# Expert results of two pairs of experts accumulated in one PSUM bank, and added to the rows after the gate and up products instead of between their steps

## The chip, the cores and the metric

The kernel runs on one core of a Trainium2 chip. Its metric is the device time in microseconds (us) of one execution. Names of engines: PE is TensorE's matmuls, PEld its weight loads, DVE is VectorE, ACT is ScalarE, POOL is GpSimd, SP is SyncE, which issues most transfers.

## What is computed

Two blocks follow each other on 512 tokens of 1024 features. The first (two layers of pooling, retention and RWKV branches) and the attention of the second are the same on both sides of the change. The change is in the mixture of experts at the end: 32 experts, of which every token uses two.

```python
def _hierarchical_moe(xt, w_rg, b_rg, w_re, b_re, w_gate, w_up, w_down):
...
    y = jnp.zeros_like(xt)
    for e in range(N_EXPERTS):
        he = jax.nn.silu(xt @ w_gate[e]) * (xt @ w_up[e])
        y = y + combine[:, e:e + 1] * (he @ w_down[e])
    return y
...
        x = x + y.reshape(B, T, D)
    return _rmsnorm(x, final_norm)
```

An expert has 1024 x 256 gate weights, as many up weights, and 256 x 1024 down weights, all float32.

## The kernel before

The experts' stage (`experts`, `pairs`) takes the last sixth of the span. The tokens were sorted to their experts beforehand: an expert has 64 places (`CAP`), and a pair of experts fills the 128 partitions, so there are n = 16 pairs. `pairs` goes over them, and PE's instructions keep the order in which the code is written (the call of `pairs` stands under `manual_schedule` for PE); for the other engines a scheduler chooses the order. For each pair p the code does this:

- `one_hots`, `places` (lines 1693 to 1701): for the pair three further on, which tokens lie at its 128 places, their weights `ws` and their rows `idx`; an indirect transfer from POOL (`rows`, line 1705) then fetches the 128 rows of 1024 features into `xg`. On PE this is four small matmuls (line 1682), on DVE the two reductions `ws` (1686) and the cast `idx` (1690).
- `gate_up` (1731): 8 steps of two matmuls (line 1737) with 64 columns of stationary operand each, one for each expert of the pair, into the halves of one bank `pp`. The trace shows each as two records, so the whole product is 32. After them tanh on ACT (1741) and two DVE instructions (1742, 1743) make the hidden values `eth`.
- `turned` (1708): four transposes (1712) and an ACT copy (1714) give `ohT`, the one-hots turned, that is, the matrix that takes an expert's places back to tokens.
- `gather` (1717): twice four transposes (1725) and a DVE multiply (1728) give `xt`, the next pair's rows with the features on the partitions. The code stops between its two halves.
- `transposed` (1746): two transposes of `eth` (1750) and an ACT copy `eht` (1752).
- `down` (1755): two halves of four matmuls (1762), 16 records in all, and for each half the weighted result in two parts, `hi` by ACT (1765) and `lo` by DVE (1766). These four tiles of 128 x 512 are the `ys` of the pair; they lie in buffers with the tag `y`.
- `add` (1769): a generator of 8 steps, one for each block of 128 tokens and each half of the features. A step is two matmuls (line 1775: `ohT` block as stationary operand, `hi` then `lo`) into one of two banks `mm`, and a DVE instruction (1777) that adds the bank to the tokens' rows `xr`.

The generator `add` of a pair is run one step at a time between the 8 steps of the next pair's `gate_up`:

```python
            for _ in self.gate_up(2 * p, x, wts):
                next(add, None)
...
            ys = list(self.down(2 * p, pl[p][1], ht, wts))
            add = self.add(oT[p], ys)
```

The last pair (p = 15) is written out behind the loop: its `gate_up` runs alone, with a branch at its fifth step (`rest`, for tokens past an expert's capacity), and the steps of pair 14's `add` stand around its `down`.

Weights come from SP's queue. Five buffers each hold an expert's gate and up weights (`eg`, 2 MB) and down weights (`ed`, 1 MB). A buffer is refilled when the products that read it are done: the refills of `eg` wait for the end of a `gate_up`, those of `ed` for the end of a `down`.

Of the kernel before, what the change touches and what calls it, by code (L numbers as in the profile page):

```python
# [33 lines left out]
# columns of the packed parameters of a layer, 128 features to a column  # L34
# [8 lines left out]
# 128-wide feature tiles of w_in, in the order in which they are used  # L43
# [21 lines left out]
# constants that follow from the shapes alone  # L65
def _consts():
# [28 lines left out]
    # for the second block  # L95
# [7 lines left out]
    # biases of the distances 511 .. -128: one-hot bucket, log of the number of dilations with the distance  # L103
# [26 lines left out]
def _groups(w, g=128):  # L130
    """[K, N] -> [128, N/g, K/128, g]"""
    K, N = w.shape
    return w.reshape(K // 128, 128, N // g, g).transpose(1, 2, 0, 3)


def _pack(a):
# [25 lines left out]
    # second block  # L162
# [17 lines left out]
class Layers:  # L180
    """The first block, with the features on the partitions and the tokens along the free axis."""

    def __init__(self, ctx, tc, a, dbg=None):
# [6 lines left out]
        # pools of the first block; those on the right side also serve the second  # L190
# [10 lines left out]
        # what only the first block needs  # L201
# [65 lines left out]
    def rsqrt(self, src, n, scale, eps, out=None, own=""):  # L267
        """(src * scale + eps) ** -0.5 on [128, n] by Newton's iteration"""
# [20 lines left out]
    def load(self, dst, src):  # L289
        """behind the loads that the start waits for"""  # L290
        if self.after is None:
            self.nc.sync.dma_start(dst, src)
        else:
            with self.tc.issue_after(self.after.ins):
                self.nc.sync.dma_start(dst, src)
# [12 lines left out]
    def mm3(self, ps, w, h, start=True, stop=True):  # L308
        """ps += w.T @ h, of parts (hi, lo): hi hi + hi lo + lo hi"""
# [8 lines left out]
    def parts(self, src, scale=1.0, tile=None):  # L318
        """hi and lo of a [128, 512] tile"""
# [11 lines left out]
    def dense(self, src, h):  # L331
        """[128 features, 512 tokens] in PSUM: src.T @ h for weights [128, k, 128] in DRAM"""
        p = self.P()
        self.mm3(p, self.split(self.load_w(src)), h)
        return p
# [28 lines left out]
    def mod_params(self):  # L364
        """silu(c) and the layers' parameters"""
# [19 lines left out]
    def mod_start(self, half):  # L385
        """the columns of silu(c) @ w_ada + b_ada that a half of the first norm's features needs"""
        nc, a = self.nc, self.a
        pc, mod, sc = self.mods[0]
        # rows of 512 columns on the partitions 0, 32 and (of every other 128 features) 64, 96, then turned into columns
# [21 lines left out]
    def mod_rest(self):  # L411
        """the other columns, a tile of features at a time"""
# [18 lines left out]
    def rstd_row(self, ss):  # L431
        """[128, 512] in PSUM: 1 / rms of the tokens, the same on all partitions; ss are parts of the sum of squares"""
# [23 lines left out]
    def modnorm(self, xs, rb, sc, sh):  # L456
        """hi and lo of x * rb * sc + sh; x is overwritten"""
# [17 lines left out]
    def rwkv_proj(self, l, h, tiles):  # L475
        """projections p + (p of the token before - p) * mu"""
# [25 lines left out]
    def both(self, *gens):  # L502
        """the generators step by step together"""
# [27 lines left out]
    def to_row(self, s):  # L531
        """[128 tokens, (block, head)] -> [4 heads, 512 tokens]"""
# [8 lines left out]
    def rwkv_prep(self, l, hf, r, k, v, wa):  # L541
        """scaled operands of the chunked recurrence"""
# [19 lines left out]
        for i in range(2):  # L562
# [27 lines left out]
            # k * (1 + (a - 1) * k_a)  # L590
# [23 lines left out]
        # half of (bonus * v + ln_b)  # L614
# [9 lines left out]
        # products of a chunk, masked, by way of DRAM: rows B|K, columns A|R; a unit is a chunk of a head  # L624
# [16 lines left out]
        # B and K times the decay from the token to the chunk's end  # L641
# [7 lines left out]
        # inverses of the diagonal blocks of 32, a block to a partition  # L649
# [27 lines left out]
    def rwkv_chain(self, l, AR, BT, v, bv, DC, gd, tn):  # L677
# [4 lines left out]
        def operands(ch):  # L682
            # operands of the chunk
# [42 lines left out]
        for ch in range(NC_):  # L726
# [10 lines left out]
            # the chunk  # L737
# [64 lines left out]
    def layernorm(self, y, g, eps, tile, own):  # L802
        """in place on [128, 512] of g groups: (y - mean) * rstd"""
# [14 lines left out]
    def silu2(self, ps):  # L818
        """2 * silu of a PSUM tile"""
# [12 lines left out]
    def branch(self, l, n, o, h, acc, gates=()):  # L832
        """acc += 2 * sigmoid(gate logits) * (o @ w_branch)"""
# [18 lines left out]
    def pool_mixer(self, l, h, pc):  # L852
        """causal window means, less the token itself; a map per group; gated"""
# [41 lines left out]
    def rows_of(self, src, h, tile, scale=None):  # L895
        """[128 tokens, 512 features] tiles of the product with four tiles of weights"""
# [27 lines left out]
    def rope_tables(self):  # L924
        """cos and signed sin of the positions times the frequencies"""
# [8 lines left out]
        # ang - 2 pi n, with 2 pi in four parts that take few bits each  # L934
# [103 lines left out]
    def layer(self, l, h, xnext):  # L1038
        """returns the next x and the sum of its squares by partition"""
# [38 lines left out]
        for d in range(8):  # L1078
# [10 lines left out]
            if l == 1:  # L1089
                ss2 = self.sumsq(ss2, x, self.pv2[:, d:d + 1])  # L1090
                # parts of x * final_g * attn_norm for the second block; its norms follow the products
# [51 lines left out]
class Second(Layers):  # L1143
    """The second block: attention, then the experts, with the tokens on the partitions."""

    def second_block(self, xs, ss, ss2, out):
# [11 lines left out]
        # norms of the two blocks' ends: rs1 of x, rs2 of x * rs1 * final_g  # L1158
# [7 lines left out]
        # rs1 = (s1 + eps) ** -0.5, rs1 * rs2 = (s2 + eps * (s1 + eps)) ** -0.5  # L1166
# [53 lines left out]
    def bcast_tokens(self, rs):  # L1220
        """[128, 512] in PSUM from [128 tokens, 4]: the same on all partitions"""
# [18 lines left out]
    def x_rows(self, xs, rs1):  # L1240
        """the first block's result with the tokens on the partitions"""
# [14 lines left out]
    def gates(self, h):  # L1256
        """-cumsum(log sigmoid(f)) of the heads, to DRAM"""
# [23 lines left out]
        # log(1 + exp(-|z|)) = 2 atanh(u), u = (1 - t) / (3 + t), t = tanh(|z| / 2)  # L1281
# [613 lines left out]
```

## Time and profile before

| | us |
|---|---|
| median of 3 runs | 2035.27 |
| fastest and slowest of them | 2031.1, 2045.47 |
| span of the profiled execution, first to last instruction | 2034.7 |

The profile gives the span of its execution and not the time of the call; of the three runs the median is the nearest, 0.57 us above that span, and this is taken as what lies around it. In the rows, "idle before" is an engine's waiting time and the arrow says what ended it; a row of the timeline merges neighbouring instructions of one kind (x16), and its start is that of the first. Matmuls are pipelined, so that the recorded durations of two neighbours overlap: how fast they follow each other is read from their starts.

### The profile page before, as it was taken

To read this page: it belongs to the slowest core of one execution; us is meant where nothing else is said; L and a number is where in the kernel's file an instruction comes from. 1 tells how busy PE (TensorE), PEld (TensorE's weight loads), DVE (VectorE), ACT (ScalarE), POOL (GpSimd) and SP (SyncE) were. 2 spreads that over 40 slices of the span, in tenths; PEclk is the share of its full clock that TensorE was granted. 3 is DMA by queue.
4 is the path that set the end of the run, shared out by engine and by line. 5 is a ranking of instruction groups with operands and counts; after the bars stand their busy time and mean duration, and the time that the engine had idled before them with its cause. 6 is when DMAs were issued, how large, how long until landed. Compare 5 with 4: busy or idle time off the path is not lost. (4 is left out here: it accounts for less than half of the span.)

```text
span 2034.7 us, 26175 instructions
## 1 busy us (share of the span) xinstructions
PE 1924.1 (95%) x10034; PEld 1399.2 (69%) x10034; DVE 1130.2 (56%) x2353; ACT 594.5 (29%) x1054; POOL 538.3 (26%) x444
## 2 busy tenths in 40 slices
PE   6899889999999989979999999999999998999996
PEld 3778667878887867767778888787787686333332
DVE  4656977763334555587674334375564545455445
ACT  3332223233322333213233323352343432111112
POOL 1342454335537411224221232310101221000000
PEclk9899889999999989989999999999999798999999
DMA  7424313443333622421233232345231245888981
GB/s 297 135 88 120 107 48 95 138 118 115 117 97 127 214 68 74 133 82 56 76 108 102 73 95 68 91 136 173 73 104 52 100 188 221 346 362 343 367 320 53
DMA packets 103127, 289.02 MB, mean 142 GB/s; under 512 B 31112, under 2 KB 44296, under 8 KB 94808
## 3 DMA queue, kind: packets, MB, share of 16 engines
q1 hardware_dynamic: 97912, 267.40, 38.7%
q0 software_dynamic: 5088, 19.93, 2.6%
q8 instruction: 80, 1.31, 0.3%
q14 instruction: 47, 0.39, 0.1%
HBM read 268.90 MB, written 21.01 MB: 142 GB/s over the span
## 5 line engine op out<-in xcount | busy, mean ns | idle before, releaser
L313 PE MATMUL mm<-hi,whi 128*128 128x512 f32 x1424 | 575.8, 405 | 26.5 <-DVE ry L966 10.5
L313 PE MATMUL mm<-hi,wlo 128*128 128x512 f32 x1424 | 568.7, 400 | 3.2 <-DVE wlo L305 2.9
L313 PE MATMUL mm<-lo,whi 128*128 128x512 f32 x1424 | 569.7, 400 | 1.6 <-DVE lo L326 1.1
L313 PEld LDWEIGHTS mm<-hi,whi 128*128 128x128 f32 x1424 | 272.1, 191 | 98.6 <-issue 12.7
L302 ACT ACTIVATE whi<-wst 128x1024 fp32r<-128x1024 f32 (+1 forms) x202 | 192.9, 957 | 487.4 <-PE mm L313 354.9
L313 PEld LDWEIGHTS mm<-hi,wlo 128*128 128x128 f32 x1424 | 272.4, 191 | 68.2 <-DVE wlo L305 5.9
L313 PEld LDWEIGHTS mm<-lo,whi 128*128 128x128 f32 x1424 | 272.7, 191 | 65.9 <-issue 6.3
L305 DVE TENSOR_TENSOR wlo<-wst,whi 128x1024 fp32r<-128x1024 f32 (+1 forms) x162 | 186.3, 1152 | 146.5 <-ACT whi L302 144.8
L305 POOL TENSOR_TENSOR wlo<-wst,whi 128x1024 fp32r<-128x1024 f32 (+1 forms) x40 | 86.4, 2161 | 355.6 <-ACT whi L302 260.9
L1737 PE MATMUL pp<-eg,xt 128*64 128x512 f32 x512 | 136.0, 618 | 0.2 <-PEq L1785 0.2
L1777 DVE TENSOR_TENSOR xr<-xr,mm 128x512 f32<-128x512 f32 x128 | 87.3, 685 | 87.0 <-PE mm L1775 86.7
L419 POOL TENSOR_TENSOR wad<-wad,cact 128x1024 f32<-128x1024 f32 x32 | 67.5, 2111 | 147.0 <-DMA wad<-wada 138.6
L1775 PEld LDWEIGHTS mm<-y,ohT 128*128 128x128 f32 x256 | 38.3, 188 | 98.8 <-DVE xr L1777 72.7
L1775 PE MATMUL mm<-y,ohT 128*128 128x512 f32 x256 | 92.5, 446 | 1.9 <-DVE xr L1777 1.9
L421 POOL TENSOR_TENSOR wad<-wad 128x512 f32<-128x512 f32 (+2 forms) x96 | 90.1, 939 | 6.0
L915 PE MATMUL mm<-vhi,hi 128*128 128x256 f32 x256 | 75.9, 301 | 6.8 <-ACT vhi L909 4.2
L1705 POOL DMA_INDIRECT xg<-hx,idx x16 | 15.5, 966 | 240.8 <-DVE oh L1552 204.1
L915 PE MATMUL mm<-vlo,hi 128*128 128x256 f32 x256 | 75.2, 296 | 0.6 <-DVE vlo L910 0.6
L915 PE MATMUL mm<-vhi,lo 128*128 128x256 f32 x256 | 74.9, 294 | 0.0
L847 POOL TENSOR_TENSOR acc<-acc,tg 128x512 f32<-128x512 f32 x32 | 49.9, 1560 | 94.2 <-DVE tg L845 65.2
L1737 PEld LDWEIGHTS pp<-eg,xt 128*64 128x64 f32 x512 | 28.3, 137 | 54.3 <-issue 54.0
L663 DVE TENSOR_TENSOR tmp<-tt,lt 64x31 f32<-64x31 f32 (+15 forms) x124 | 57.4, 463 | 6.1 <-DMA lt<-gd 3.6
(409 smaller groups left out, 2858.3 us busy)
## 6 DMA issues: line engine op xcount, KB each, us to landing
wst<-win SPq DMA_DIRECT2D x154, 512.0 KB, 3.8
eg<-egu SPq DMA_DIRECT2D x31, 2048.0 KB, 13.5
ed<-edn SPq DMA_DIRECT2D x31, 1024.0 KB, 11.0
wad<-wada SPq DMA_DIRECT2D x48, 512.0 KB, 4.8
wst<-wbr SPq DMA_DIRECT2D x48, 256.0 KB, 2.8
gd<-gs SPq DMA_DIRECT2D x64, 128.0 KB, 1.9
gt<-gd SPq DMA_DIRECT2D x32, 256.0 KB, 3.1
wst<-wout SPq DMA_DIRECT2D x16, 512.0 KB, 4.1
```

The lines of the kernel that those rows point to most:

```text
L302: nc.scalar.activation(hi, w, AF.Copy)
L305: e.tensor_tensor(lo, w, hi.bitcast(F32), op=OP.subtract)
L313: self.nc.tensor.matmul(ps, w[x][:, k, :], h[y][k], start=start and k == 0 and i == 0, stop=stop and k == n - 1 and i == 2)
L419: nc.gpsimd.tensor_tensor(w, w, self.cact.unsqueeze(2).to_broadcast([128, 8, 128]), op=OP.mult)
L421: nc.gpsimd.tensor_add(w[:, :n], w[:, :n], w[:, n:2 * n])
L663: nc.vector.tensor_tensor(t, tt[:, 0:j + 1, j:j + 1].to_broadcast([2 * nu, j + 1, n]), lt[:, j:j + 1, j + 1:].to_broadcast([2 * nu, j + 1, ...
L847: nc.gpsimd.tensor_add(acc[d], acc[d], t)
L915: nc.tensor.matmul(p[:, :256], h[x][k][:, tb * 128:tb * 128 + 128], parts[y][k // 2][:, k % 2, :], start=k == 0 and i == 0, stop=k == 7 an ...
L1705: self.last_row = self.nc.gpsimd.indirect_dma_start(xg, None, self.hx[:, :], bass.IndirectOffsetOnAxis(ap=idx, axis=0))
L1737: nc.tensor.matmul(p[64 * i:64 * i + 64], x[:, k, 64 * i:64 * i + 64], wts[e + i][0][:, k], start=k == 0, stop=k == 7)
L1775: nc.tensor.matmul(p, oT[:, 128 * tb:128 * tb + 128], y, start=i == 0, stop=i == 1)
L1777: nc.vector.tensor_tensor(xr, xr, p, op=OP.add)
```

## The change

Results of two pairs, p - 1 and p with p odd, are added together. A step of `add` now has four matmuls into one bank (hi and lo of the one pair, hi and lo of the other) and still one DVE instruction. The 8 steps of such a double are taken four at a time, with all of them behind `gate_up`, `places` and the first half of `gather`: four in the next pair (first half of the features), four in the one after it (second half). Pair 14 takes all eight steps of pairs 12 and 13. The results of pairs 14 and 15 are added by themselves around and behind the last pair's `down`, as before. `turned` moves behind the add steps. The `y` buffers go from 6 to 8, the `eth` buffers from 2 to 1. Comments and docstrings are left out too, and line numbers from 1642 on move by 4 to 6 (1737 is 1741 after the change, 1775 is 1781, 1777 is 1783).

```diff
-        add = iter(())
+        add, ys = iter(()), []
         for p in range(n - 1):
             if p + 3 < n:
                 oh = self.one_hots(p + 3)
             for _ in self.gate_up(2 * p, x, wts):
-                next(add, None)
+                pass
             ht = self.hidden
             if p + 3 < n:
                 pl.append(self.places(p + 3, oh))
-            if p:
-                oT.append(self.turned(pl[p + 1][0]))
             x = self.gather(pl[p + 1])
             next(x)
+            for _ in range(4 if p < n - 2 else 8):
+                next(add, None)
+            if p:
+                oT.append(self.turned(pl[p + 1][0]))
             ht = self.transposed(ht)
             x = next(x)
-            ys = list(self.down(2 * p, pl[p][1], ht, wts))
-            add = self.add(oT[p], ys)
+            ys.append(list(self.down(2 * p, pl[p][1], ht, wts)))
+            if p % 2:
+                add = self.add(zip(oT[p - 1:p + 1], ys[p - 1:p + 1]), True)
             if p == n - 3:
                 self.flag = nc.values_load(self.flag[0:1, 0:1], min_val=0, max_val=T)
+        add = self.add([(oT[n - 2], ys[n - 2])])
...
-        for _ in self.add(oT[p], ys, True):
+        for _ in self.add([(oT[p], ys)], True):
             pass
...
-        th = self.S("eth", [128, 256], "eth", 2)
+        th = self.S("eth", [128, 256], "eth", 1)
...
-            hi, lo = (self.S("y", [128, 512], "y", 6, F32R) for _ in range(2))
+            hi, lo = (self.S("y", [128, 512], "y", 8, F32R) for _ in range(2))
...
-    def add(self, oT, ys, halves=False):
+    def add(self, pairs, halves=False):
+        pairs = list(pairs)
         for tb, c in sorted(((tb, c) for tb in range(4) for c in range(2)), key=lambda i: i[::-1] if halves else i):
             p = self.P()
-            for i, y in enumerate(ys[c]):
-                nc.tensor.matmul(p, oT[:, 128 * tb:128 * tb + 128], y, start=i == 0, stop=i == 1)
+            parts = [(oT, y) for oT, ys in pairs for y in ys[c]]
+            for i, (oT, y) in enumerate(parts):
+                nc.tensor.matmul(p, oT[:, 128 * tb:128 * tb + 128], y, start=i == 0, stop=i == len(parts) - 1)
             xr = self.xr[tb][:, 512 * c:512 * c + 512]
             nc.vector.tensor_tensor(xr, xr, p, op=OP.add)
             yield
```

The order of PE's instructions shows where the add steps stand. Before the change, around the end of one pair's gate and up products (`pp`), the last step of the previous pair's adds (`mm`) follows the last products, and the small matmuls of the next pair's preparation come behind it:

```order
L1737 MATMUL pp_15042<-eg_14043,xt_15004 64x512
L1737 MATMUL pp_15042<-eg_14047,xt_15004 64x512
L1775 MATMUL mm_15087<-y_15036,ohT_14892 128x512
L1775 MATMUL mm_15087<-y_15037,ohT_14892 128x512
L1682 MATMUL ms_15095<-cwx_13543,oh_15040 128x6 x4
L1712 MATMUL rm_15107<-ident,oh_14820 128x128 x4
L1725 MATMUL rm_15115<-ident,xg_14885 128x128 x4
L1750 MATMUL qy_15121<-ident,eth_15091 128x128 x2
L1725 MATMUL rm_15126<-ident,xg_14885 128x128 x4
```

After the change, at the same place on PE, the products end without an add, the preparation comes first, and then the first of four add steps, now of four matmuls with two `ohT`:

```order
L1741 MATMUL pp_15064<-eg_14051,xt_14995 64x512
L1741 MATMUL pp_15064<-eg_14055,xt_14995 64x512
L1686 MATMUL ms_15085<-cwx_13543,oh_15062 128x6 x4
L1729 MATMUL rm_15098<-ident,xg_14891 128x128 x4
L1781 MATMUL mm_15104<-y_14854,ohT_14725 128x512
L1781 MATMUL mm_15104<-y_14855,ohT_14725 128x512
L1781 MATMUL mm_15104<-y_14956,ohT_14827 128x512
L1781 MATMUL mm_15104<-y_14957,ohT_14827 128x512
```

Three more such steps follow it on PE, into the banks `mm_15110`, `mm_15116` and `mm_15122`, and only then the turned one-hots, the transposes of `eth`, the second half of the gather and the down products:

```order
L1781 MATMUL mm_15122<-y_14956,ohT_14827 128x512
L1781 MATMUL mm_15122<-y_14957,ohT_14827 128x512
L1716 MATMUL rm_15128<-ident,oh_14858 128x128 x4
L1754 MATMUL qy_15135<-ident,eth_15081 128x128 x2
L1729 MATMUL rm_15140<-ident,xg_14891 128x128 x4
L1766 MATMUL ms_15146<-ed_14052,eht_15138 64x512
```

On DVE, before the change, the additions to `xr` stand between the steps and the last one between the two instructions that make `eth`:

```order
L1777 TENSOR_TENSOR xr_11110<-xr_11110,mm_14641 128x512
L1742 SCALAR_TENSOR_TENSOR eth_14651<-eth_14651,pp_14602 128x256
L1777 TENSOR_TENSOR xr_11110<-xr_11110,mm_14647 128x512
L1686 TENSOR_REDUCE ws_14660<-ms_14655 64x1 x2
L1743 TENSOR_TENSOR eth_14651<-eth_14651,pp_14602 128x256
L1690 CAST idx_14663<-ms_14655 128x1
L1552 TENSOR_TENSOR oh_14710<-pm_13542,cst_10905 128x512
L1728 TENSOR_TENSOR xt_14674<-rm_14675,pv_82 128x512
```

After the change DVE makes `ws`, `idx`, the first half of `xt` and `eth` first, and the four additions of the pair stand together behind them:

```order
L1690 TENSOR_REDUCE ws_14682<-ms_14677 64x1
L1746 SCALAR_TENSOR_TENSOR eth_14673<-eth_14673,pp_14656 128x256
L1690 TENSOR_REDUCE ws_14682<-ms_14677 64x1
L1694 CAST idx_14685<-ms_14677 128x1
L1732 TENSOR_TENSOR xt_14689<-rm_14690,pv_82 128x512
L1747 TENSOR_TENSOR eth_14673<-eth_14673,pp_14656 128x256
L1783 TENSOR_TENSOR xr_11107<-xr_11107,mm_14696 128x512
L1783 TENSOR_TENSOR xr_11108<-xr_11108,mm_14702 128x512
L1783 TENSOR_TENSOR xr_11109<-xr_11109,mm_14708 128x512
L1783 TENSOR_TENSOR xr_11110<-xr_11110,mm_14714 128x512
L1552 TENSOR_TENSOR oh_14756<-pm_13542,cst_10905 128x512
L1732 TENSOR_TENSOR xt_14689<-rm_14732,pv_82 128x512
```

The transfers keep their order on SP and POOL, and ACT's instructions keep theirs.

## Rows read from the trace of the kernel before

**Rows 1.** Busy time by engine, granted clock, DMA share and GB/s, 50 us of the stage.

```profile
1850.00:1900.00 50.00, 49.01 (x216) 19.10 (x216) 25.95 (x49) 6.84 (x13) 2.80 (x3) 1.00 0.86 340
```

**Rows 2.** Costliest groups: line, engine, names, count, busy and mean ns, idle before and releasers.

```profile
L1777 DVE TENSOR_TENSOR xr<-xr,mm 128x512 f32<-128x512 f32 x128 | 87.3, 685 | 87.0 <-PE mm L1775 86.7
L1775 PEld LDWEIGHTS mm<-y,ohT 128*128 128x128 f32 x256 | 38.3, 188 | 98.8 <-DVE xr L1777 72.7
L1775 PE MATMUL mm<-y,ohT 128*128 128x512 f32 x256 | 92.5, 446 | 1.9 <-DVE xr L1777 1.9
```

**Rows 3.** Timeline of one pair, down product to down product: start, length, engine, line.

```profile
1840.66 3.65 PE L1762 MATMUL ms<-ed,eht 128*64 128x512 f32 x16
...
1844.14 1.03 PE L1737 MATMUL pp<-eg,xt 128*64 128x512 f32 x4
...
1845.10 0.73 PE L1775 MATMUL mm<-y,ohT 128*128 128x512 f32 x2
...
1845.77 1.08 PE L1737 MATMUL pp<-eg,xt 128*64 128x512 f32 x4
...
1846.77 0.73 PE L1775 MATMUL mm<-y,ohT 128*128 128x512 f32 x2
...
1857.39 0.50 PE L1682 MATMUL ms<-cwx,oh 128*128 128x6 f32 x4
...
1857.75 0.66 PE L1712 MATMUL rm<-ident,oh 128*128 128x128 f32 x4
...
1858.24 0.60 PE L1725 MATMUL rm<-ident,xg 128*128 128x128 f32 x4
...
1858.44 0.60 ACT L1714 ACTIVATE ohT<-rm 128x512 fp32r<-128x512 f32 x1 [1.10 <-PE rm L1712]
...
1859.14 0.44 PE L1750 MATMUL qy<-ident,eth 128*128 128x128 f32 x2 [0.29 <-DVE eth L1743]
...
1859.61 0.38 ACT L1752 ACTIVATE eht<-qy 128x256 f32<-128x256 f32 x1 [0.57 <-PE qy L1750]
...
1860.05 2.37 PE L1762 MATMUL ms<-ed,eht 128*64 128x512 f32 x10
```

**Rows 4.** Timeline of PE in the dense products: first and twelfth of 12 neighbours.

```profile
1484.04 0.39 PE L313 MATMUL mm<-lo,whi 128*128 128x512 f32 x1
...
1486.54 0.39 PE L313 MATMUL mm<-hi,whi 128*128 128x512 f32 x1
```

**Rows 5.** Timeline of PE in the last pair: two add steps without a product between.

```profile
2010.92 1.19 PE L1775 MATMUL mm<-y,ohT 128*128 128x512 f32 x4
...
2012.04 1.94 PE L1762 MATMUL ms<-ed,eht 128*64 128x512 f32 x8
```

**Rows 6.** Timeline behind pair 0's gate and up products, which have no adds.

```profile
1720.81 0.61 PE L1682 MATMUL ms<-cwx,oh 128*128 128x6 f32 x4
...
1721.28 0.66 PE L1725 MATMUL rm<-ident,xg 128*128 128x128 f32 x4
...
1722.82 0.41 DVE L1743 TENSOR_TENSOR eth<-eth,pp 128x256 f32<-128x256 f32 x1
...
1724.25 3.65 PE L1762 MATMUL ms<-ed,eht 128*64 128x512 f32 x16
```

**Rows 7.** As rows 1, while transfers stream without a gap.

```profile
1744.00:1758.00 14.00, 14.00 (x56) 4.12 (x52) 6.17 (x9) 1.37 (x2) 0.41 (x1) 1.00 1.00 417
```

**Rows 8.** SP's issues of weights in the timeline, and their landing from the page.

```profile
1837.52 0.80 SPq L1613 DMA_DIRECT2D eg<-egu  x2
...
1856.91 0.81 SPq L1613 DMA_DIRECT2D eg<-egu  x2
...
eg<-egu SPq DMA_DIRECT2D x31, 2048.0 KB, 13.5
```

**Rows 9.** As rows 1, before pair 0's products and in the wait behind them.

```profile
1710.40:1715.40 5.00, 4.97 (x16) 2.57 (x18) 1.38 (x2) 0.00 (x0) 0.41 (x1) 0.51 0.99 363
...
1722.00:1723.00 1.00, 0.00 (x0) 0.00 (x0) 0.99 (x4) 0.00 (x0) 0.00 (x0) 1.00 0.83 164
```

More of the change, by code (lines that the diff above doesn't have):

```diff
@@ L1649, in pairs @@
                 pl.append(self.places(p + 3, oh))
+            x = self.gather(pl[p + 1])
+            next(x)
+            for _ in range(4 if p < n - 2 else 8):
+                next(add, None)
             if p:
                 oT.append(self.turned(pl[p + 1][0]))
-            x = self.gather(pl[p + 1])
-            next(x)
             ht = self.transposed(ht)
             x = next(x)
-            ys = list(self.down(2 * p, pl[p][1], ht, wts))
-            add = self.add(oT[p], ys)
+            ys.append(list(self.down(2 * p, pl[p][1], ht, wts)))
+            if p % 2:
+                add = self.add(zip(oT[p - 1:p + 1], ys[p - 1:p + 1]), True)
             if p == n - 3:
                 self.flag = nc.values_load(self.flag[0:1, 0:1], min_val=0, max_val=T)
+        add = self.add([(oT[n - 2], ys[n - 2])])
         p = n - 1
```

## The prediction, made before the changed kernel was run

> **What bounds the kernel now.** I read the busy time by stretches first. In the experts' stage PE is busy 49.0 of 50 us at a granted clock of 1.00, DVE 26.0 and ACT 6.8, and the DMA engines carry 0.86 of what they can [rows 1]. So PE sets the pace and the transfers run close behind it. The costliest groups come next [rows 2]. DVE's additions look expensive (128 of them, 87.3 us, and 87.0 us of waiting before them), but it is DVE that waits for PE. PE's weight loads show 72.7 us of waiting "for DVE", yet the matmuls themselves waited 1.9 us for it: a load that stands behind a running product has nothing to do, and the row names the last event it saw. Taking additions off DVE is therefore worth nothing by itself. What counts is how close together PE's instructions stand, and for that I read the timeline of one pair by its start times [rows 3].
>
> A pair takes 19.39 us, from one down product to the next (1840.66 to 1860.05). The down product is 16 records in 3.48 us (1840.66 to 1844.14), 0.2175 us each. A step of the gate and up product is 4 records of the same shape, so 0.87 us alone. But a step together with its add step takes 1.67 us (1845.10 to 1846.77): 0.67 for the two adds (to 1845.77) and 1.00 for the four records. Two matmuls of the add's shape (128x128 stationary, 512 columns) need far less when they follow each other: eleven of them take 2.50 us in the dense products, 0.2275 each [rows 4]. So a step should cost 0.87 + 0.455 = 1.325, and the other 0.35 us is the price of going from one tile shape to the other and back, eight times per pair. The last pair shows it from the other side: four adds in a row take 1.12 us (2010.92 to 2012.04) [rows 5], which is 4 x 0.2275 plus 0.21 for going in and out.
>
> **The change part by part.** Matmuls: 224 add matmuls run in the loop before and after, 16 per pair on average. Nothing is removed on PE; what goes is the alternation. DVE loses 56 of 128 additions, 56 x 0.685 = 38 us of busy time, all of it beside PE's work: counted as 0.
>
> Now one pair from 2 to 13, with the end of the gate and up product as zero. The products take 2 x 3.48 = 6.96 us without the adds. The small matmuls of the next places start at once, the first half of the gather at 0.47 (1720.81 to 1721.28 where no add stood in between [rows 6]); four transposes take 0.49 (1857.75 to 1858.24 [rows 3]), so the adds start at 0.96. A step is 4 x 0.2275 = 0.91, with 0.10 once for going in: steps end at 1.97 and 2.88. The third step needs the first bank back. DVE has the two `eth` instructions, `ws`, `idx` and `xt` queued ahead of its additions; in pair 0 that chain ended 2.42 after the products (1722.82 + 0.41 - 1720.81 [rows 6]). So the first addition runs from 2.42 to 3.10, PE waits 0.22, steps three and four end at 4.05 and 4.96, and the second bank (free at 3.79) holds up nothing. A DVE addition takes 0.69 against 0.91 for a step, so DVE does not become the pace.
>
> This wait is new. Behind it on PE stand `turned`, the transposes of `eth`, the second half of the gather and the down product. `eth` is long ready by then, so today's wait for it (0.29 on PE [rows 3]) goes. But `turned` now stands directly before the transposes, and on ACT its copy `ohT` stands before `eht`: `ohT` starts 0.69 after the transposes (1857.75 to 1858.44) and takes 0.60, so `eht` starts at 4.96 + 0.69 + 0.60 = 6.25 at the earliest, and the down product 0.44 after that (1859.61 to 1860.05), at 6.69. The pair takes 6.96 + 6.69 + 3.48 = 17.13 us, 2.26 less than now; 12 pairs give 27.1.
>
> Pair 1 loses its adds altogether. Its tail is that of pair 0, 3.44 from the products to the down product (1720.81 to 1724.25 [rows 6]), so 13.88 in place of 19.39: 5.5 gained. Pair 14 has eight steps: 17.13 + 16 x 0.2275 = 20.77, 1.4 lost. The last pair's program is the same. Sum: 27.1 + 5.5 - 1.4 = 31.2 us, to be taken from the profiled execution's own time, 2034.7 of span and 0.6 around it, which is the median of the runs: 2004.1 us.
>
> What I cost at nothing: the `y` buffers (the next pair's four results fit into the four that its first-half adds have just freed, so ACT and DVE do not wait for later adds; without that cover the additions would wait behind `lo` on DVE), and the single `eth` buffer (its last reader is a whole product away from its next writer). `oh` and the second half of `xt` stand behind the four additions on DVE, some 2.8 us later than today, covered by the 3.48 us of the down product and the first four steps of the next one. The indirect fetch from POOL is issued after `idx`, which stays ahead of the additions, and its rows are wanted two pairs later. On SP the order stays; the `eg` refills are issued at the end of the products, which now comes some 6 us earlier within the pair.
>
> **Whether the weights keep up** is the term that no row shows directly, because today they wait for PE. A pair moves 2 x 2048 + 2 x 1024 KB of weights and 512 KB of rows, 6.82 MB; at 417 GB/s, measured over 14 us with the engines full [rows 7], that is 16.4 us. From the other side, 340 GB/s at a share of 0.86 [rows 1] makes 395 when full, 17.25 us, which is 0.1 over my pair. Refills issued at 1856.91 land 13.5 later, 1870.4 [rows 8]; the product that needs them starts 2 x 19.39 behind 1844.14, at 1882.9. That lead of 12.5 us covers 12 x 0.1. I take no loss, and keep the other end for the range.
>
> The Trainium skill ("DMA: Bandwidth & Descriptors", Where 436 GB/s comes from) speaks against this: it holds that loads from HBM are bound at about 358 GB/s per core, which by an estimate from that figure would be 19.05 us per pair, hardly below today. The trace does not bear it out: 417 GB/s stand in rows 7.
>
> **Rivals.** (1) The weights set the pace. If the transfers cannot do better on average than today's 6.82 MB in 19.39 us (352 GB/s), pair 14 can start only as much earlier as the lead allows, 12.5, minus 1.4: 2024 us; if they do slightly better, 18.6 us per pair (366 GB/s), another 9 us come: 2015. I put this case at 2020. For it: the share of 0.86. Against it: rows 7. (2) Standing together does not help: the adds keep 0.33 us each, as between the products now. Then a pair's adds take 5.3 instead of 3.6 us, the 12 pairs gain 0.6 each, pair 14 loses 4.7: 7 + 5.5 - 4.7 = 8, so 2027. For it: the add reloads 128 columns of `ohT` for every matmul. Against it: rows 4 do so too, at 0.2275, and rows 5. (3) Slower than before: the clock. PE's new waits in each pair (0.22 for the bank, about 0.5 for `eht`) make the granted clock fall at each pair, and it comes back only after some 5 us of work, as at the stage's start, where it was 0.51, the lower of the two levels, over 5.0 us [rows 9]. That loses 5.0 x 0.49 = 2.45 us in each of 14 pairs, 34.3 in all: 2004.1 + 34.3 = 2038. It decides from 31.2 / 14 = 2.2 us per pair on. Against it: pair 0 has a wait of over a microsecond at the same place (1722 to 1723, PE not busy at all) at a clock of 1.00 [rows 9], and the products behind it ran at full pace.
>
> The Trainium skill ("TensorE: Matmul & The Clock Gate", A second HAM failure mode) describes rival 3: a PE that idles briefly between groups while it cycles through PSUM banks can swing between its two clocks. By that rule the result would be the 2038 of rival 3; rows 9 show no fall behind a longer wait, so I give it little.
>
> **How the numbers follow.** Forecast 0.76, weights 0.10, no gain from standing together 0.07, clock 0.07. The forecast's own range: with neither the bank's wait (0.22) nor that for `eht` (0.33) it is 12 x 0.55 = 6.6 lower, 1997.5; with DVE's chain 1 us later than in pair 0 it is 12 higher, 2016. The three runs lie within 0.7% of each other, so about 1% (20 us) is what a measurement of this kernel can tell from no change. The range 1996 to 2016 takes in the forecast and the better end of rival 1. Faster by over 1% (below 2015): nearly all of the forecast and a third of rival 1, 0.78. Within 1%: the rest of rival 1, rival 2 and most of rival 3, 0.17. Slower by over 1%, if the clock stays low for longer than 5 us per pair: 0.05.
>
> **What would show it.** SP's `eg` refills come every 17.1 us instead of 19.4; between two of them 32 product records take about 7.0 us, 16 add matmuls about 3.9; the additions' count is 72. A wait of PE on a transfer within the products means rival 1, add records 0.33 apart within a step mean rival 2, a granted clock below 1.00 between 1750 and the last pair rival 3. PE waiting for DVE at every add step, and not only at the third, would make the forecast wrong in its largest term.

## The result, and the profile after

The changed kernel takes 2006.69 us (median of 4 runs, 2002.31 to 2011.46) against 2037.9 us (4 runs, 2031.1 to 2045.47) for the kernel before beside it: a ratio of 0.9844, 95% interval 0.9814 to 0.9875. The profiled execution took 2007.01 us, 2005.2 of it span. The prediction was 2004.1 us in 1996 to 2016. The two medians differ by 31.2 us, to the digit what was forecast; that closeness is luck, since executions of one kernel lie up to 14 us apart (2031.1 to 2045.47).

The busy time by stretches, in the columns of [rows 1], for two stretches of the stage after the change:

```profile
1750.00:1800.00 50.00, 48.74 (x244) 24.32 (x242) 21.20 (x42) 7.89 (x15) 2.81 (x3) 1.00 1.01 424
...
1850.00:1900.00 50.00, 48.71 (x244) 24.27 (x242) 21.18 (x42) 7.88 (x15) 2.81 (x3) 1.00 0.99 402
```

PE is no busier than in [rows 1] (48.7 of 50 us, before 49.0), but it gets through 244 matmul records in the time in which it got through 216. The clock stays at 1.00. DVE falls from 26.0 to 21.2. The transfers have gone from a share of 0.86 to about 1.00: in the same time they bring more weights, and that stands nearly at what they can do.

The costliest groups, which answer to [rows 2], and the landing of the weights, which answers to [rows 8] (from the page):

```profile
L1781 PE MATMUL mm<-y,ohT 128*128 128x512 f32 x256 | 69.2, 409 | 3.2 <-DVE xr L1783 1.6
...
L1781 PEld LDWEIGHTS mm<-y,ohT 128*128 128x128 f32 x256 | 44.8, 188 | 23.3 <-DVE xr L1783 13.2
...
eg<-egu SPq DMA_DIRECT2D x31, 2048.0 KB, 14.4
```

The 256 add matmuls are all still there, at 69.2 us of busy time instead of 92.5. The idle time before their weight loads fell from 98.8 to 23.3 us, but that is not what was gained: the matmuls themselves show 1.9 us of waiting before and 3.2 now, a little more. A refill of weights takes 0.9 us longer to land (14.4 against 13.5).

One pair in the timeline, which answers to [rows 3]:

```profile
1843.17 3.65 PE L1766 MATMUL ms<-ed,eht 128*64 128x512 f32 x16 [0.31 <-ACT eht L1756]
...
1846.66 7.04 PE L1741 MATMUL pp<-eg,xt 128*64 128x512 f32 x32
...
1853.62 0.61 PE L1686 MATMUL ms<-cwx,oh 128*128 128x6 f32 x4
...
1854.50 4.33 PE L1781 MATMUL mm<-y,ohT 128*128 128x512 f32 x16
...
1855.97 1.34 DVE L1783 TENSOR_TENSOR xr<-xr,mm 128x512 f32<-128x512 f32 x2
1856.71 1.69 PEld L1781 LDWEIGHTS mm<-y,ohT 128*128 128x128 f32 x8 [0.55 <-DVE xr L1783]
...
1858.67 0.60 PE L1716 MATMUL rm<-ident,oh 128*128 128x128 f32 x4
...
1859.31 0.60 ACT L1718 ACTIVATE ohT<-rm 128x512 fp32r<-128x512 f32 x1 [5.16 <-PE rm L1716]
...
1859.80 0.38 ACT L1756 ACTIVATE eht<-qy 128x256 f32<-128x256 f32 x1
...
1860.23 1.08 PE L1766 MATMUL ms<-ed,eht 128*64 128x512 f32 x4 [0.31 <-ACT eht L1756]
```

A pair takes 17.06 us (1843.17 to 1860.23) where it took 19.39. The 32 product records follow each other for 6.96 us, and the 16 add matmuls stand in one block. What holds the block up is seen in the loads: the second eight start at 1856.71, right behind DVE's first addition (1855.97 + 0.69 = 1856.66), which frees their bank. Then `ohT` and `eht` follow on ACT, and the down product waits 0.31 us for `eht`.

SP's first issue of an `eg` refill stands at the end of pair 0's products, and the program ahead of it is the same in both kernels. Of before, the timeline of SP's queue:

```profile
1720.91 1.06 SPq L1613 DMA_DIRECT2D eg<-egu  x2
```

and of after:

```profile
1723.65 1.06 SPq L1613 DMA_DIRECT2D eg<-egu  x2
...
1751.43 0.80 SPq L1613 DMA_DIRECT2D eg<-egu  x2
...
1921.91 0.33 SPq L1613 DMA_DIRECT2D eg<-egu  x1
```

From this refill to the end of the span before took 2034.7 - 1720.91 = 313.8 us, after 2005.2 - 1723.65 = 281.55: the stage gained 32.2 us. The profiled execution gained only 29.5, since its unchanged first part happened to be 2.7 us longer. I call this length the stage below, and the distance of two refills the period ((1921.91 - 1751.43) / 10 = 17.05 us after the change). In all the kernels here but the one with full tiles (whose pair 0 itself takes longer) the start of the stage lies anywhere from 1713.95 to 1729.85, up to 16 us apart, so a single run's total says little and these two say much. Stage and period are of one profiled execution each; where no number of runs is given below, the kernel was run once.

### The profile page after: what moved, and what is told of

It is laid out like the page before. It is cut to its first block, busy times and chain, and to the rows that moved or that the text cites. A ratio compares the mean times of both kernels' runs of the same rounds, so it can differ in the third digit from the quotient of the medians.

```text
span 2005.2 us, 26106 instructions
## 1 busy us (share of the span) xinstructions
PE 1897.0 (95%) x10034; PEld 1417.7 (71%) x10034; DVE 1092.4 (54%) x2297; ACT 592.9 (30%) x1054; POOL 539.2 (27%) x444
## 5 line engine op out<-in xcount | busy, mean ns | idle before, releaser
L1741 PE MATMUL pp<-eg,xt 128*64 128x512 f32 x512 | 114.6, 600 | 0.2 <-PEq L1791 0.2
L1741 PEld LDWEIGHTS pp<-eg,xt 128*64 128x64 f32 x512 | 37.1, 139 | 74.5 <-issue 74.2
L1781 PE MATMUL mm<-y,ohT 128*128 128x512 f32 x256 | 69.2, 409 | 3.2 <-DVE xr L1783 1.6
L1766 PE MATMUL ms<-ed,eht 128*64 128x512 f32 x256 | 58.7, 599 | 4.2 <-ACT eht L1756 4.0
L1781 PEld LDWEIGHTS mm<-y,ohT 128*128 128x128 f32 x256 | 44.8, 188 | 23.3 <-DVE xr L1783 13.2
## 6 DMA issues: line engine op xcount, KB each, us to landing
eg<-egu SPq DMA_DIRECT2D x31, 2048.0 KB, 14.4
```

What stands on the lines that cost most here:

```text
L1741: nc.tensor.matmul(p[64 * i:64 * i + 64], x[:, k, 64 * i:64 * i + 64], wts[e + i][0][:, k], start=k == 0, stop=k == 7)
L1766: nc.tensor.matmul(py[64 * i:64 * i + 64], ht[:, 128 * k + 64 * i:128 * k + 64 * i + 64], wts[e + i][1][:, k, 512 * c:512 * c + 512], star ...
L1781: nc.tensor.matmul(p, oT[:, 128 * tb:128 * tb + 128], y, start=i == 0, stop=i == len(parts) - 1)
```

## The experiments

My theory: what costs is PE going from one tile shape to the other and back, 0.35 us each time, eight times per pair before the change and once now; and four matmuls per bank keep DVE off the pace. Seven times 0.35 is 2.45 us per pair, of which 19.39 - 17.05 = 2.34 are seen. Rivals: the gain comes from fewer additions on DVE; or from where the block stands; or weights, not PE, set the period by now.

**The move alone.** Two matmuls per bank as before, but all eight add steps behind the products:

```diff
             for _ in self.gate_up(2 * p, x, wts):
-                next(add, None)
+                pass
...
-            if p:
-                oT.append(self.turned(pl[p + 1][0]))
             x = self.gather(pl[p + 1])
             next(x)
+            for _ in add:
+                pass
+            if p:
+                oT.append(self.turned(pl[p + 1][0]))
```

> Only the place changes: each pair's 8 add steps of two matmuls stand together behind the gate and up products, and every step keeps its own DVE addition. If the alternation of tile shapes is all that cost time, a pair takes the 17.05 us of the changed kernel. My theory has a second half: 8 additions of 0.67 us behind a DVE chain that ends 2.4 us after the products let the bank of the last step free only at about 6.4, so the adds end near 6.9 and not 5.05, and a pair takes about 18.9 us, some 2028 us in all. If only the number of additions counts, a pair stays at 19.4.

2028.14 us (before beside it 2036.03), period 19.30, stage 2026.4 - 1714.20 = 312.2 us: 1.6 us gained and no more. The direction is the one expected, but a pair takes 0.4 us more than the 18.9 expected; that the total meets the expected 2028 is luck, as this run's stage began 6.7 us earlier than that of the kernel before. PE and DVE in the timeline of this kernel:

```profile
1846.88 1.33 PE L1777 MATMUL mm<-y,ohT 128*128 128x512 f32 x4 [1.03 <-DVE xr L1779]
1848.39 1.33 PE L1777 MATMUL mm<-y,ohT 128*128 128x512 f32 x4 [0.18 <-DVE xr L1779]
...
1846.14 1.28 DVE L1779 TENSOR_TENSOR xr<-xr,mm 128x512 f32<-128x512 f32 x2
1847.65 1.29 DVE L1779 TENSOR_TENSOR xr<-xr,mm 128x512 f32<-128x512 f32 x2 [0.22 <-PE mm L1777]
```

The alternation is gone, and DVE takes its place: PE waits for it at every second step, and DVE in turn waits 0.22 us for PE, since only two banks go round. Two additions come every 1.51 us (1846.14 to 1847.65), 0.755 each and not the 0.67 of my expectation, while two matmuls take 0.455. With four matmuls per bank PE needs 0.91 and is the slower of the two again. So the move pays only together with the merging.

**Merged, but between the products.** The changed kernel with its four-matmul steps behind every second step of the products:

```diff
-            for _ in self.gate_up(2 * p, x, wts):
-                pass
+            for k, _ in enumerate(self.gate_up(2 * p, x, wts)):
+                if k % 2 or p == n - 2:
+                    next(add, None)
...
-            for _ in range(4 if p < n - 2 else 8):
-                next(add, None)
```

> Only the merging: add steps of four matmuls for two pairs, but between the gate and up steps, one behind every second step (pair 14: behind every step). My theory: four alternations of 0.35 us less per pair, 19.39 - 1.4 = 18.0 us, and the wait for eth stays; some 2018 us in all. If the number of DVE additions counts, 17.1 us as in the changed kernel. If the place behind the products is what counts, 19.4.

2026.96 us, period 18.00, stage 2025.2 - 1729.85 = 295.4 us, 18.4 less than before. The period is what the theory gives; the total is high because this run's stage began 9 us later than that of the kernel before. PE in its timeline:

```profile
1845.34 1.21 PE L1780 MATMUL mm<-y,ohT 128*128 128x512 f32 x4
...
1848.35 1.21 PE L1780 MATMUL mm<-y,ohT 128*128 128x512 f32 x4
...
1854.47 0.66 PE L1728 MATMUL rm<-ident,xg 128*128 128x128 f32 x4 [0.39 <-DVE xt L1731]
```

From one add step to the next it is 3.01 us: 8 x 0.2175 + 4 x 0.2275 = 2.65, and 0.36 for one change of shape and back. The wait that is left behind the products is another than I expected: PE waits 0.39 us for `xt`, the first half of the gather, and not 0.29 for `eth`.

**As many additions, half the alternations.** The kernel before, with two of its add steps behind every second step of the products:

```diff
-            for _ in self.gate_up(2 * p, x, wts):
-                next(add, None)
+            for k, _ in enumerate(self.gate_up(2 * p, x, wts)):
+                if k % 2:
+                    next(add, None)
+                    next(add, None)
```

> The kernel before with two add steps behind every second gate and up step in place of one behind each: as many additions and as many matmuls, half the alternations. My theory: the same 18.0 us per pair as with merged steps between the products (some 2016 us in all); the additions, 0.69 us each and two for every 3.1 us, do not pace it. If the additions count, 19.4 us.

2004.71 us, period 17.63, stage 2002.9 - 1713.95 = 289.0 us, 24.8 less than before. Its timeline and its busy time (columns of [rows 1]):

```profile
1846.00 1.20 PE L1777 MATMUL mm<-y,ohT 128*128 128x512 f32 x4
...
1849.00 1.20 PE L1777 MATMUL mm<-y,ohT 128*128 128x512 f32 x4
```

```profile
1850.00:1900.00 50.00, 49.90 (x235) 22.28 (x234) 27.29 (x53) 8.22 (x15) 2.80 (x3) 1.00 0.96 385
```

The group takes 3.00 us again, with two banks and two additions in it. DVE makes as many additions per pair as before the change, and is at 27.3 of 50 us: the number of additions does not count, which fells that rival. The period is 0.37 below my 18.0; most of that is the 0.29 us wait for `eth` [rows 3], which is gone from PE, as the last two steps cover the chain that makes it. This kernel is one small edit (two lines become four) and gets three quarters of the stage's gain; its total equals the changed kernel's only because its first part was 9.7 us shorter.

**One tile shape for all.** The kernel before, alternating as ever, but with products that use all 128 columns of the stationary matrix (both experts' products go into one bank, so the values are others):

```diff
-                nc.tensor.matmul(p[64 * i:64 * i + 64], x[:, k, 64 * i:64 * i + 64], wts[e + i][0][:, k],
-                                 start=k == 0, stop=k == 7)
+                nc.tensor.matmul(p, x[:, k], wts[e + i][0][:, k], start=k == 0 and i == 0, stop=k == 7 and i == 1)
```

> The kernel before with gate and up products that use all 128 columns of stationary operand (the tokens of both experts of the pair against the weights of each, summed in one bank: other values than the reference's), so that products and adds have one tile shape. Products get longer; what counts is a step with its add step against a step alone in the same run (pairs 0 and 15) plus 0.455. If the change of tile shape is what costs 0.35 us, that difference falls to 0.05 or less. If any change of the kind of matmul (float32 to float32r) costs it, it stays at 0.3 to 0.4.

2134.34 us, as its products take about twice as long each. Its weight loads in the timeline, and one row of PE: around one step (L1774 is the add), and then, late in the run, the first and the last of nine neighbours without adds:

```profile
1869.69 0.19 PEld L1774 LDWEIGHTS mm<-y,ohT 128*128 128x128 f32 x1 [0.24 <-issue]
1870.36 0.41 PEld L1737 LDWEIGHTS pp<-eg,xt 128*128 128x128 f32 x2
1870.58 1.88 PE L1737 MATMUL pp<-eg,xt 128*128 128x512 f32 x4
...
1871.87 0.19 PEld L1774 LDWEIGHTS mm<-y,ohT 128*128 128x128 f32 x1 [0.24 <-issue]
...
2090.20 0.19 PEld L1737 LDWEIGHTS pp<-eg,xt 128*128 128x128 f32 x1 [0.24 <-issue]
...
2093.63 0.19 PEld L1737 LDWEIGHTS pp<-eg,xt 128*128 128x128 f32 x1 [0.24 <-issue]
```

Alone, such a product takes (2093.63 - 2090.20) / 8 = 0.429 us. Four of them and two adds make 4 x 0.429 + 2 x 0.2275 = 2.17, and a step takes 2.18 (1869.69 to 1871.87). Alternating costs nothing here, 0.35 where the shapes differ. The change from float32 products to float32r adds is still there, so that rival falls. The loads of the kernel before show where the two part:

```profile
1845.76 0.20 PEld L1737 LDWEIGHTS pp<-eg,xt 128*64 128x64 f32 x4 [0.36 <-issue]
1846.77 0.30 PEld L1775 LDWEIGHTS mm<-y,ohT 128*128 128x128 f32 x2 [0.81 <-issue]
```

There each load for the other shape starts with its matmul (1845.76 and 1845.77, 1846.77 and 1846.77 [rows 3]); with one shape the product's load behind the adds starts 0.22 us ahead of its matmul (1870.36 and 1870.58), so that part of it lies under the matmuls before. The Trainium skill ("TensorEngine Tiling (Array Packing)", Key Properties) states that a change of the tiling mode drains TensorE. The traces agree that such a change costs time, 0.35 us there and back; that a drain is what costs it, no run here shows. What this experiment does not separate: its products also take twice as long, which leaves more cover for a load, so the tile shape as the cause rests on this one run with that reserve, while the price itself does not. Add matmuls cut to 64 columns, which would test it without that, were not tried.

**No adds at all.** The changed kernel without the add steps of pairs 0 to 13, whose results stay out of the output:

```diff
-            for _ in range(4 if p < n - 2 else 8):
-                next(add, None)
```

> The changed kernel without the add steps of pairs 0 to 13, so their results are left out of the output: what PE would then ask of the weights. PE alone needs the 13.9 us of pair 1 per pair. If the transfers have no limit near, pairs take 13.9 us throughout. My estimate: 6.82 MB per pair at 417 GB/s are 16.4 us, so after some five pairs on the lead of 12.5 us a pair takes 16.3 to 16.5 us and PE waits for a transfer. If the limit is near 352 to 366 GB/s, 18.6 to 19.4 us.

1970.41 us. The first five pairs take 13.9 us, and after three more the period is 16.1 (1829.18 to 1893.61 is four of them), a little under the 16.3 to 16.5 expected. PE, and the busy time:

```profile
1839.12 7.08 PE L1739 MATMUL pp<-eg,xt 128*64 128x512 f32 x30 [1.23 <-DMA eg<-egu]
```

```profile
1850.00:1900.00 50.00, 43.39 (x206) 16.88 (x204) 12.98 (x30) 8.42 (x16) 2.81 (x3) 1.00 1.01 424
```

Here the weights do set the pace: PE waits for `eg` inside the products, at 424 GB/s. That is the floor for this stage, 16.1 us per pair. The changed kernel stands 1 us above it and PE shows no such wait there, so weights are not its limit.

**The turn ahead of the adds.** In the changed kernel `turned` moves in front of the gather and the adds, so that `ohT` no longer stands between the adds and `eht` on ACT:

```diff
+            if p:
+                oT.append(self.turned(pl[p + 1][0]))
             x = self.gather(pl[p + 1])
             next(x)
             for _ in range(4 if p < n - 2 else 8):
                 next(add, None)
-            if p:
-                oT.append(self.turned(pl[p + 1][0]))
```

> The changed kernel with the turned one-hots ahead of the gather and the adds, where they stood before the change. My theory of what is left in a pair: PE waits 0.43 us for a bank before the third add step and 0.31 for eht, which stands behind ohT on ACT. With ohT made earlier and the adds starting 0.49 later, both go: 17.05 becomes 16.5 to 16.6 us per pair, 12 pairs and pair 14 give 6 to 7 us against the changed kernel, and a ratio of about 0.981 to the kernel before. The weights do not stop it (16.07 us per pair is the shortest that they allowed without adds). Rival: the second half of the gather then waits for the first half's copy, as in the run with merged steps between the products, and the pair stays at 17.0.

2007.28 us (6 runs, 1991.99 to 2008.41), ratio 0.9833, 0.9803 to 0.9863; period 16.98, stage 279.5. A miss: PE no longer shows a wait for `eht`, but little is gained, 0.07 us per pair where 0.5 was expected. PE, DVE and ACT in its timeline:

```profile
1839.09 0.61 PE L1686 MATMUL ms<-cwx,oh 128*128 128x6 f32 x4
...
1840.52 0.68 DVE L1552 TENSOR_TENSOR oh<-pm,cst 128x512 fp32r<-128x512 f32 x1
...
1842.05 1.28 DVE L1783 TENSOR_TENSOR xr<-xr,mm 128x512 f32<-128x512 f32 x2
...
1842.78 2.12 PE L1781 MATMUL mm<-y,ohT 128*128 128x512 f32 x8 [0.27 <-DVE xr L1783]
...
1844.47 0.60 ACT L1718 ACTIVATE ohT<-rm 128x512 fp32r<-128x512 f32 x1 [4.86 <-PE mm L1781]
...
1845.59 1.94 PE L1766 MATMUL ms<-ed,eht 128*64 128x512 f32 x8
```

The turn is the last reader of the one-hot matrix whose buffer the next one takes. Moved up, it frees that buffer early, and DVE, whose order the scheduler chooses, builds the next one (`oh`, 0.68 us) ahead of the additions. The first addition starts 2.96 us after the products instead of 2.35, PE waits for the bank, and most of what ACT gave, DVE took. The edit also moved the copy `ohT` on ACT in every second pair only: in the pair shown, it still starts behind the adds (1844.47), as it waits for them to give back one of the four `ohT` buffers.

**The changed kernel again**, beside it on the same chip:

> The changed kernel once more, beside the one with the turned one-hots first, on the same chip: 17.05 us per pair, a ratio of 0.984 to the kernel before. If the whole gain lies in the experts' stage, the stretch from the first refill of eg to the end of the span stays at 281.5 us, 32 less than before, while the part ahead of it moves by some us from run to run.

2006.73 us (5 runs, 2005.04 to 2010.1), ratio 0.9856, 0.9831 to 0.988; period 17.05, stage 281.6: both are as in the first profiled execution of this kernel.

**The one-hot behind the additions.** The kernel with the turn ahead, and the one-hot matrix for a later pair made one pair earlier, tied behind the last addition:

```diff
+        oh = self.one_hots(3)
...
-            if p + 3 < n:
-                oh = self.one_hots(p + 3)
             for _ in self.gate_up(2 * p, x, wts):
...
             for _ in range(4 if p < n - 2 else 8):
                 next(add, None)
+            if p + 4 < n:
+                with self.tc.issue_after(self.last_add.ins) if p > 1 else nullcontext():
+                    oh = self.one_hots(p + 4)
...
-            nc.vector.tensor_tensor(xr, xr, p, op=OP.add)
+            self.last_add = nc.vector.tensor_tensor(xr, xr, p, op=OP.add)
```

> The run with the turn moved ahead of the additions, and in addition the one-hot matrix of a later pair is built on VectorE behind the last addition of the pair instead of ahead of the first one (made one pair earlier, so it is there when TensorE wants it). Theory (in the previous run it was VectorE's place for that 0.68 us instruction that held the first addition until 2.96 us after the products, so that TensorE waited 0.27 us for a bank, the additions ended 5.64 us after the products and the down product began 6.50 after them): the first addition on VectorE starts about 2.28 us after the products, its bank is free at 2.96, TensorE wants it at 1.32 + 1.82 = 3.14, so no wait for xr in front of L1783's matmuls is left, the four steps run 1.32 to 4.96 and the down product starts near 5.9; period 16.4 us (16.3 to 16.6) against 16.98, first refill to end of span 272.5 to 275 us against 279.5 there and 281.6 in the changed kernel, and the total some 0.3 to 0.5% under the changed kernel's apart from the part ahead of the stage. Rival 1 (the weights bind already this close to their 16.07 us per pair): a wait on eg or ed appears in front of the products and the period stays near 16.9. Rival 2 (VectorE's second half of the gather, now behind the one-hot, makes the next pair's products late): a wait for xt of 0.5 us or so in front of the products, period 17.0 as before.

2003.54 us (5 runs, 1995.77 to 2004.23), ratio 0.9809, 0.9788 to 0.9829; period 16.56, stage 2002.5 - 1727.13 = 275.4 us. PE, its loads and DVE in the timeline:

```profile
1854.21 0.61 PE L1688 MATMUL ms<-cwx,oh 128*128 128x6 f32 x4
...
1855.50 1.67 PEld L1783 LDWEIGHTS mm<-y,ohT 128*128 128x128 f32 x8
1856.72 0.69 DVE L1785 TENSOR_TENSOR xr<-xr,mm 128x512 f32<-128x512 f32 x1
1857.46 1.69 PEld L1783 LDWEIGHTS mm<-y,ohT 128*128 128x128 f32 x8 [0.29 <-DVE xr L1785]
...
1860.34 0.20 PEld L1768 LDWEIGHTS ms<-ed,eht 128*64 128x64 f32 x4 [0.34 <-ACT eht L1758]
```

No wait of PE for the gather's second half and none for weights has come in its place, and the period lies inside the 16.3 to 16.6 expected; the stage is 0.4 us over the 275 expected. The first addition starts 2.51 us after the products and not 2.28, so the bank still holds the loads a little: the second eight come 1.96 us after the first eight (1855.50 to 1857.46) where four matmuls twice need 1.82, and the down product starts 6.13 after the products (1860.34) where 5.9 was expected. By stage this version is below both kernels, 6.2 us less than the changed one. In whole times the step is about 0.3 to 0.5%, and its interval (up to 0.9829) overlaps that of the changed kernel's first comparison (from 0.9814), so it rests on the stage's length and the period, each of one profiled execution.

The periods side by side: before 19.39, move alone 19.30, merged between the products 18.00, two steps at a time 17.63, the change 17.05, turn ahead 16.98, one-hot behind as well 16.56, no adds 16.1.

## Why the prediction was right, point by point

**The price of alternating** (0.35 us per step) was the largest term, and it holds: 0.36 and 0.35 with half as many alternations, nothing with one tile shape (whose products take twice as long).

**The chain behind the products**, each time after their end (1853.62):

| | predicted | measured |
|---|---|---|
| adds start | 0.96 | 0.88 |
| DVE's first addition starts | 2.42 | 2.35 |
| third step starts | 3.10 | 3.09 |
| adds end | 4.96 | 5.05 |
| `ohT` starts on ACT | 5.65 | 5.69 |
| `eht` starts on ACT | 6.25 | 6.18 |
| down product starts | 6.69 | 6.61 |

All times agree to 0.09 us. Part of that is two errors that cancel: steps three and four take 1.96 us instead of 1.82, and `eht` starts 0.49 after `ohT` instead of 0.60. The forecast's own steps from 3.10 on (0.91 each) end at 4.92 and not at the 4.96 that it has, and its rival 3 puts the wait for `eht` at about 0.5 where its range has 0.33; measured are 0.31.

**The sum.** A pair takes 17.05 us by the period (predicted 17.13). Counted one by one, a pair runs from the down product of the pair ahead of it to its own. In the timeline of before, the down products of pairs 1, 13 and 14 (pair 0's is in [rows 6]) are:

```profile
1743.70 1.51 PE L1762 MATMUL ms<-ed,eht 128*64 128x512 f32 x6
...
1976.04 3.65 PE L1762 MATMUL ms<-ed,eht 128*64 128x512 f32 x16
...
1995.03 3.65 PE L1762 MATMUL ms<-ed,eht 128*64 128x512 f32 x16
```

In the timeline of after, those of pairs 0, 1, 13 and 14 are these, with the rows of pair 14's adds:

```profile
1726.99 3.65 PE L1766 MATMUL ms<-ed,eht 128*64 128x512 f32 x16
...
1740.89 3.65 PE L1766 MATMUL ms<-ed,eht 128*64 128x512 f32 x16
...
1945.05 3.65 PE L1766 MATMUL ms<-ed,eht 128*64 128x512 f32 x16 [0.31 <-ACT eht L1756]
...
1955.50 0.66 PE L1729 MATMUL rm<-ident,xg 128*128 128x128 f32 x4
1955.91 8.22 PE L1781 MATMUL mm<-y,ohT 128*128 128x512 f32 x32
1963.97 0.60 PE L1716 MATMUL rm<-ident,oh 128*128 128x128 f32 x4
...
1965.53 3.65 PE L1766 MATMUL ms<-ed,eht 128*64 128x512 f32 x16 [0.31 <-ACT eht L1756]
```

Pair 1 takes 13.90 (predicted 13.88) where it took 19.45, so 5.55 are gained. The 12 pairs from 2 to 13 take 204.16 in place of 232.34, 28.18 gained (predicted 27.1, as each pair was put 0.08 too long). Pair 14 takes 20.48 in place of 18.99, 1.49 lost. Together 5.55 + 28.18 - 1.49 = 32.24, which is the stage's gain; 31.2 were predicted. For pair 14 the forecast had 20.77 in place of 19.39: both are too long by 0.3 to 0.4, because a pair that has no `places` left to do (13 and 14) was already shorter before, which I had not counted, and now its adds start 0.41 after the products and not 0.88. The two errors cancel, and the loss of 1.4 came out nearly right.

The stage did 1.0 us better than forecast, and yet the median lies 2.6 us above the forecast. The changed kernel's profiled execution (2007.01) adds up: its first part was 2.7 us longer than that of the trace I started from, and the time lies 1.8 us above the span (2007.01 - 2005.2) where I had taken 0.57, so that 2004.1 + 1.2 + 2.7 - 1.0 = 2007.0.

**The covers** held: DVE's busy time went from 1130.2 to 1092.4 us (56 x 0.685 = 38) with no gain to be seen from it (two steps at a time keep all additions and gain 24.8 us of stage), and between 1745 and 1950 us no wait of PE for `y`, `oh` or `xt` came up.

**The rivals.** Weights: no wait for them, at 402 to 424 GB/s with a lead that suffices; the floor they would set is 16.1 us, a little under my 16.4 to 17.25. The 358 GB/s of the Trainium skill ("DMA: Bandwidth & Descriptors", Where 436 GB/s comes from), for which I had worked out 19.05 us per pair, were exceeded here. The Trainium skill ("HBM Reference", Specifications (TRN2)) also gives about 425 for a core that streams alone, and the traces agree with 424; whether the neighbouring core was idle, no run here shows. No gain from standing together: 32 adds in a row take 8.06 us (1955.91 to 1963.97), 0.25 each with the bank waits in it, and not 0.33. The clock: 1.00 in both stretches with two short waits in each pair, so nothing of rival 3's 34 us came.

## What to carry to other kernels

Count how often TensorE goes from one tile shape to another, not only its matmuls: here each there-and-back cost as much as one and a half matmuls, and batching two steps already got three quarters of the gain. Before batching, compare the time to fill a bank with the time to empty it: two matmuls (0.455 us) against 0.755 on VectorE moved the bound and gained only 1.6 us in all, four (0.91) keep TensorE busy. And when a step moves, ask which buffer it frees, since a scheduler may fill the free place with work in front of what is now critical.

## What the runs showed that I had not expected

- Where PE and DVE wait for each other's banks, a 128x512 addition takes more than its own time: 0.755 us each with two banks in turn, against 0.685 for the instruction itself and some 0.6 from one start to the next where two stand ready (1.28 for two).
- The weights' transfers reach 424 GB/s over 50 us with PE and DVE at work beside them, at a share of 1.01.
- The start of the stage, behind 1.7 ms whose program is the same in all these kernels, moved by up to 16 us between profiled executions (1713.95 to 1729.85); what moves it stays open. Half of the whole gain of this change is lost in that if single totals are compared.
